# A hybrid mLSTM and Hyena block: MLP operand places opened from the start, the first mLSTM head begun beside the last value projections, and a new order from the mLSTM to the output projection

## The chip, the cores and the metric

The kernel runs on one core of a Trainium2 chip. A time is the device time of one execution in microseconds (us). The unchanged kernel took 2704.43 us, the median of three runs between 2702.84 and 2706.27.

## What is computed

One layer of an encoder on a sequence of 2048 rows and width 1024, in float32:

```python
hn = rms_norm(x, norm_mix_pre)
proj = hn @ w_in
cv = short_conv3(proj[..., :N_CONV], conv_w, conv_b)        # 2560 columns
q, k = heads(silu(cv[..., :512])), heads(silu(cv[..., 512:1024])) * 128 ** -0.5
v, o_gate = heads(proj[..., 2560:3072]), sigmoid(proj[..., 3072:3584])
gates = proj[..., 3584:3600] + b_gates                      # log i, log f, two directions, 4 heads
h_fwd = mlstm_chunkwise(q, k, v, gates[:, 0], log_sigmoid(gates[:, 1]))
h_bwd = flip(mlstm_chunkwise(flip(q), flip(k), flip(v), flip(gates[:, 2]), log_sigmoid(flip(gates[:, 3]))))
y_m = group_rms((h_fwd + h_bwd) * o_gate, 4, mlstm_norm_w)  # 512 columns
z = cv[..., 1024:1536]
for o in (0, 1):                                            # Hyena, FFT over twice the length
    z = cv[..., 1536 + 512 * o:2048 + 512 * o] * two_sided_fft_conv(z, filt[:, 0, o], filt[:, 1, o], fb[o])
y_h = group_rms(z, 8, hyena_norm_w)                         # 512 columns
x = x + rms_norm(concatenate([y_m, y_h]) @ w_out, norm_mix_post)
ff = square(relu(rms_norm(x, norm_mlp_pre) @ w_mlp_in)) @ w_mlp_out
x = x + rms_norm(ff, norm_mlp_post)
```

The mLSTM has 4 heads of 128 columns. It works in chunks of 128 rows, 16 to a head. Per chunk it needs a 128x128 score (q times k), weighted by an exponential of gate sums and masked to one side per direction; the product of these weights with v; and the product of q with a state that is carried from chunk to chunk, forwards and backwards.

## The kernel before

Every dense product in float32 is made of three matmuls on rounded parts (`mm3`, lines 159 to 161): an operand is split into a high and a low part (`split`, lines 166 on ScalarE and 169 on VectorE or GpSimd). The mLSTM's and the transposes' matmuls take plain float32, and the trace shows them as two matmuls each.

The stages in order of time: the normalised input is transposed and split into `hn` (16 tiles of rows, in four blocks of four); the convolved projections; the filters' spectra; then two things at once, the values' projection (four groups of 260 columns, 16 row tiles each, `values_project`) and the Hyena convolution (`hyena`). `drive(work, leads)` interleaves these two by costs: each step of the lead yields a number, and the values advance until their own yields have reached it. When the Hyena steps are done, `long_conv` closes its pools, opens the pools of the mLSTM (`mearly`, `mps0`), loads k, v and q of head 0, yields 14, waits until the gates are computed and turns the four groups of k (`turned`, line 945: four transposes; lines 950 and 952: weighted by the gates on ScalarE and VectorE into `kw`). All this stands in a manual schedule: the engines run in the written order.

Then comes `mlstm`, whose order a scheduler sets from the written one, by its own costs. After 15 `state_step`s of head 0 (line 966: two matmuls into `pv`; line 971: the state `st`, decayed, plus `pv`), 64 chunks run, head by head. `scores` makes `pS` (line 990) and two exponentials on ScalarE (line 993) of a tile `mb`, which is a broadcast row from memory, masked on GpSimd (lines 980 and 981). After every fourth chunk line 996 forms the weights `pm` of four chunks on VectorE. Five chunks later (LAG) `values` makes `ps` (q times state, line 1008) and `pa` (weights times v, line 1010). ScalarE scales `ps` into `nm` (1015), VectorE adds `pa` (1018), and after four chunks VectorE forms a quotient (1024 to 1026), GpSimd multiplies and adds the directions (1028 and 1030), and a DMA issued by ScalarE stores `ht` to `ym`. Such later pieces are put on a list and issued by `issue` in later chunks. In chunks 6 to 9 of a head the next head's k is turned, in chunks 8 to 15 its states are stepped, two a chunk.

From chunk 50 on, `loads_ahead` loads what the output projection needs first: rows of Hyena's output for row tile 0 and later 1, and the rows k = 4..7 of `w_out` into four buffers `wf4`..`wf7`, then k = 0..3. `first_gate` gates, norms and turns row tile 0 near the end.

`out_proj` is a generator over 16 row tiles. Before its loop it turns `w_out` into operands (`weight(k)`: line 1342 on ScalarE, 1343 on VectorE, with the norm's weights). A row tile needs `po`, two banks and 48 matmuls in all: 24 of the k = 4..7 half with Hyena's row (`gate`: line 1290 `py`, lines 1291 to 1300; turned by line 1306 into `yz`) and 24 of the k = 0..3 half with the mLSTM's row (`mixed`: load `ymt`, product with the output gate at line 1371, norm; turned into `ym`). `mixed(0)` must wait for the store of the mLSTM's last chunk. The MLP follows; of its operand places (tags `hm10` to `hm71`, 8 KB per partition each) those from `hm30` on lie in a pool that opens after the mLSTM.

The queue of DMAs issued by SyncE (SP) holds the loads in written order (`load`, line 231); ScalarE issues the stores (line 234), and waits there itself until the data are ready.

## Time and profile before

| | |
|---|---|
| median of three runs | 2704.43 us |
| the profiled execution | 2700.58 us |
| its span | 2698.5 us |
| PE, PEld, DVE, ACT, POOL busy | 96%, 78%, 57%, 46%, 45% |
| last value matmul begins | 1023.39 |
| first mLSTM output matmul (`ps`) | 1043.93 |
| last mLSTM output matmuls (`pa`) begin | 1166.82 |
| first turn of an mLSTM row (`ptp`) | 1193.72 |

PE is TensorE's matmuls, PEld its weight loads, DVE VectorE, ACT ScalarE, POOL GpSimd, SP SyncE; ACTq and SPq are their DMA queues. The last four rows are positions in the profiled execution, in us from the start of its span. A row of the timeline gives start, duration, engine, line, operation, and in brackets how long the engine had been idle and what it waited for. The duration of a matmul's record is longer than the distance of starts, since matmuls overlap in a pipeline; prices come from starts.

### The profile page before, as it was taken

The numbers are of one execution on the slowest core, as the hardware profiler recorded it, in microseconds if no ns is written. First come the engines' busy times: TensorE is split into PE (matmuls) and PEld (weight loads), VectorE is DVE, ScalarE is ACT, GpSimd is POOL, SyncE is SP. The second block draws the span as 40 slices with busy tenths as digits, with TensorE's granted clock in tenths as the row PEclk, the third lists the DMA queues.
The fourth block names the chain that finished last, engine by engine and source line by source line (L and its number), as shares of the span: only waits on it lengthen the run. The fifth ranks groups of instructions, "written<-read, shape, count | busy, mean of one in ns | idle before, by whom it ended". The sixth has DMA issues, their size and how long they took to land.

```text
span 2698.5 us, 35390 instructions
## 1 busy us (share of the span) xinstructions
PE 2598.6 (96%) x12237; PEld 2109.2 (78%) x12237; DVE 1541.0 (57%) x2454; ACT 1230.1 (46%) x2292; POOL 1206.1 (45%) x964
## 2 busy tenths in 40 slices
PE   6999999999999998879997999999999999999998
PEld 4778888777798888757774788868888888888876
DVE  5676653777556666656556444474444433543477
ACT  6355544555544446643334444454544333232344
POOL 1211114555225543456667877687772340301232
PEclk9999999999999999899999999999999999999999
DMA  6233336666676658546755444555447453445555
GB/s 173 56 93 110 113 117 216 187 196 187 198 237 180 197 167 272 183 152 213 245 186 210 156 141 163 185 190 172 144 156 282 146 181 98 129 144 160 183 168 214
DMA packets 288354, 465.74 MB, mean 173 GB/s; under 512 B 37542, under 2 KB 149414, under 8 KB 287152
## 3 DMA queue, kind: packets, MB, share of 16 engines
q1 hardware_dynamic: 227600, 324.85, 39.0%
q10 hardware_dynamic: 53264, 117.53, 11.4%
q0 software_dynamic: 7312, 21.11, 3.1%
q8 instruction: 97, 1.59, 0.2%
q14 instruction: 81, 0.66, 0.1%
HBM read 289.27 MB, written 174.13 MB: 172 GB/s over the span
## 4 chain that ended last, share of the span: by engine, by line
PE 39%; DVE 4%; POOL 4%; issue 3%; DMA 2%; ACT 2%; ACTq 0%; DVEq 0%; SPq 0%; POOLq 0%
PE pm L159 13%; PE pm L160 13%; PE pm L161 13%; DMA m<-in_w_mlp_out_dram 1%; POOL xt L1255 1%; DVE cb L169 1%; POOL cb L169 1%; ACT xo L1395 1%; DVE hm L1892 0%; DVE hm L169 0%; DVE xo L1398 0%; DMA hm<-ht 0%; DVE gss L1297 0%; POOL ht L1430 0%; DVE hm L1822 0%
## 5 line engine op out<-in xcount | busy, mean ns | idle before, releaser
L166 ACT CAST cb<-m 128x1024 fp32r<-128x1024 f32 (+1 forms) x342 | 277.4, 846 | 441.3 <-PE pm L159 386.2
L169 DVE TENSOR_TENSOR cb<-m,cb 128x1024 fp32r<-128x1024 f32 (+1 forms) x222 | 237.3, 1106 | 303.1 <-ACT cb L166 302.6
L160 PE MATMUL pm<-cb 128*128 128x512 f32 x880 | 343.4, 390 | 7.8 <-DVE cb L169 7.8
L159 PE MATMUL pm<-cb 128*128 128x512 f32 x880 | 342.3, 389 | 1.3 <-DVE cb L169 1.0
L159 PE MATMUL pm<-hm,cb 128*128 128x512 f32 x840 | 331.4, 394 | 12.3 <-DVE m L1703 6.4
L161 PE MATMUL pm<-cb 128*128 128x512 f32 x880 | 342.5, 389 | 0.0
L160 PE MATMUL pm<-hm,cb 128*128 128x512 f32 x840 | 330.2, 393 | 2.5 <-POOL hm L169 2.5
L161 PE MATMUL pm<-hm,cb 128*128 128x512 f32 x840 | 329.7, 393 | 0.0
L169 POOL TENSOR_TENSOR cb<-m,cb 128x1024 fp32r<-128x1024 f32 x120 | 266.1, 2230 | 57.5 <-ACT cb L166 57.5
L1703 DVE TENSOR_TENSOR m<-pm,m 128x512 f32<-128x512 f32 x224 | 153.9, 690 | 229.4 <-PE pm L161 220.5
L159 PE MATMUL pt<-hn,w 128*128 128x512 f32 x640 | 269.5, 421 | 1.0 <-ACT hn L486 0.9
L160 PE MATMUL pt<-hn,w 128*128 128x512 f32 x640 | 253.9, 397 | 0.7 <-DVE hn L487 0.7
L161 PE MATMUL pt<-hn,w 128*128 128x512 f32 x640 | 253.0, 395 | 0.0
L169 POOL TENSOR_TENSOR raw<-raw,hi 128x512 fp32r<-128x512 f32 x160 | 206.1, 1301 | 99.7 <-ACT hi L166 74.8
L160 PEld LDWEIGHTS pm<-cb 128*128 128x128 f32 x880 | 165.2, 188 | 45.7 <-DVE cb L169 11.7
L159 PEld LDWEIGHTS pm<-hm,cb 128*128 128x128 f32 x840 | 159.2, 189 | 49.0 <-POOL cb L169 7.6
L159 PEld LDWEIGHTS pm<-cb 128*128 128x128 f32 x880 | 165.1, 188 | 36.5 <-ACT junk L1877 1.4
L161 PEld LDWEIGHTS pm<-cb 128*128 128x128 f32 x880 | 165.2, 188 | 33.9
L160 PEld LDWEIGHTS pm<-hm,cb 128*128 128x128 f32 x840 | 159.4, 190 | 37.4 <-POOL hm L169 2.9
L161 PEld LDWEIGHTS pm<-hm,cb 128*128 128x128 f32 x840 | 159.2, 190 | 34.2
L1707 ACT ACTIVATE m<-m 128x512 f32<-128x512 f32 x128 | 80.7, 630 | 229.1 <-DVE m L1703 221.7
L635 POOL DMA_DIRECT2D vp<-vst x96 | 61.2, 642 | 231.7 <-ACT vst L631 230.6
(320 smaller groups left out, 5725.6 us busy)
## 6 DMA issues: line engine op xcount, KB each, us to landing
ga<-m ACTq DMA_DIRECT2D x96, 512.0 KB, 3.6
m<-ga SPq DMA_DIRECT2D x96, 512.0 KB, 3.8
d<-st ACTq DMA_DIRECT2D x64, 512.0 KB, 3.2
m<-in_w_mlp_in_dram SPq DMA_DIRECT2D x64, 512.0 KB, 5.7
m<-in_w_mlp_out_dram SPq DMA_DIRECT2D x114, 256.0 KB, 4.0
raw<-d SPq DMA_DIRECT2D x96, 256.0 KB, 2.9
xt<-in_x_dram SPq DMA_DIRECT2D x32, 512.0 KB, 3.9
dk<-kst SPq DMA_DIRECT2D x32, 512.0 KB, 4.0
```

What stands on the lines that cost most here:

```text
L159: pe.matmul(ps, w[1], x[0], start=first, stop=False)
L160: pe.matmul(ps, w[0], x[1], start=False, stop=False)
L161: pe.matmul(ps, w[0], x[0], start=False, stop=last)
L166: self.act.copy(hi, src)
L169: (eng_lo or self.dve).tensor_tensor(lo, src, hi.bitcast(F32), ALU.subtract)
L635: pool.dma_start(dst[:, 8 * b + e:8 * b + 8:2, cc:cc + 128], st[64 * e:64 * e + 64])
L1255: eng.tensor_tensor(res[:, cs], tmp[e], res[:, cs], ALU.add)
L1395: act.activation(x1, xt, AF.Square, accum_out=ss1[:, h:h + 1])
L1703: dve.tensor_tensor(dst, a, b, ALU.add)
L1707: act.activation(g, g, AF.Relu)
```

## The change

The pool `hq` of the MLP's places with tags 40 to 71 (eight of the fourteen; `hm30` and `hm31` go to a pool that opens later) is opened at the beginning. The first two blocks of `hn` live in those places, as halves of [128, 4, 512], so that `hn_tile`, `block` and `transpose_split` index halves. When these blocks have been read for the last time, during the last group of values, the places take head 0's and head 1's k, v, q and part of the `mb` tiles. Small constant tiles share one tile `cw` (`decay` among them).

During the last values group, steps t = 4 to 15 issue these loads and the masks of the first two `mb`. After Hyena (whose yields go from 1.3 to 1.2), `long_conv` yields 1.4 after each of: four turns, 15 state steps and four scores of head 0. The value matmuls between two of these number twelve.

`mlstm` runs under a manual schedule, begins at chunk 4, and gets written tables for its loads, turns, gates, and weights. The product `pm` is issued one chunk later than its last exponential, `scaled` at once. The four operands of `w_out` k = 4..7 are made inside head 3, from one buffer `wf` in place of four. Row tiles 0 and 1 are both gated there.

The border's order is written too: operands k = 0..3 alternate with the po of row tiles 0 and 1 (k = 4..7), then the po of row tile 2, then the first mLSTM row is turned.

VectorE from the values to the mLSTM (z is Hyena's; kw, st, pm belong to head 0, or to head 1 where kw follows pm), before:

```order
L1155 TENSOR_TENSOR z<-z,pu 128x512
L952 TENSOR_TENSOR kw_10341<-ptk,qt 128x512
L952 TENSOR_TENSOR kw_10353<-ptk,qt 128x512
L971 SCALAR_TENSOR_TENSOR st<-st,decay,pv 128x129 x3
L952 TENSOR_TENSOR kw_10365<-ptk,qt 128x512
L971 SCALAR_TENSOR_TENSOR st<-st,decay,pv 128x129 x5
L952 TENSOR_TENSOR kw_10377<-ptk,qt 128x512
L971 SCALAR_TENSOR_TENSOR st<-st,decay,pv 128x129 x22
L996 SCALAR_TENSOR_TENSOR pm<-pS,mb 128x1024
```

The same place, after:

```order
L1196 TENSOR_TENSOR z<-z,pu 128x512
L976 TENSOR_TENSOR kw_10134<-ptk,qt 128x512
L976 TENSOR_TENSOR kw_10160<-ptk,qt 128x512
L976 TENSOR_TENSOR kw_10185<-ptk,qt 128x512
L976 TENSOR_TENSOR kw_10212<-ptk,qt 128x512
L995 SCALAR_TENSOR_TENSOR st<-st,cw,pv 128x129 x30
L1030 SCALAR_TENSOR_TENSOR pm<-pS,hm_10084 128x1024
```

All four groups of kw now precede the first state.

ScalarE where the operands of w_out are made (wo and hm are the operands, ht the mLSTM's output), before:

```order
L1015 ACTIVATE nm<-ps,qt 128x129 x6
L234 DMA ym<-ht 128x4x128
L1015 ACTIVATE nm<-ps,qt 128x129 x2
L1342 ACTIVATE wo_11960<-wf_10390,yw 128x1024
L166 CAST y_10396<-pty 128x512
L1342 ACTIVATE wo_11960<-wf_10391,yw 128x1024
L1295 ACTIVATE rda<-yz 128x512
L234 DMA ym<-ht 128x4x128
L1342 ACTIVATE wo_11962<-wf_10392,yw 128x1024
L1342 ACTIVATE wo_11962<-wf_10393,yw 128x1024
```

The same operands, after:

```order
L1336 ACTIVATE hm_11366<-wf,yw 128x1024
L1027 ACTIVATE mb<-mb,qt 128x128 x2
L1055 ACTIVATE nm<-ps,qt 128x129 x2
L1027 ACTIVATE mb<-mb,qt 128x128 x2
L1055 ACTIVATE nm<-ps,qt 128x129 x2
L1336 ACTIVATE hm_11366<-wf,yw 128x1024
L234 DMA ym<-ht 128x4x128
L1027 ACTIVATE mb<-mb,qt 128x128 x2
L1055 ACTIVATE nm<-ps,qt 128x129 x2
L1027 ACTIVATE mb<-mb,qt 128x128 x2
L1055 ACTIVATE nm<-ps,qt 128x129 x2
L1336 ACTIVATE hm_11368<-wf,yw 128x1024
```

They stood behind the last scaling of the mLSTM and now stand between the exponentials and scalings of its last head.

SP's queue of loads in head 3, before (rd, xg, rda: Hyena's rows; mb: rows of the weights; wf, wfa: rows of w_out):

```order
L231 DMA rd_10394<-d_3601 128x2x512
L231 DMA xg_10395<-vp_76 128x1x512
L231 DMA wf_10390<-in_w_out_dram 128x1024
L231 DMA mb<-mrow 128x2x512
L231 DMA wf_10391<-in_w_out_dram 128x1024
L231 DMA mb<-mrow 128x2x512
L231 DMA wf_10392<-in_w_out_dram 128x1024
L231 DMA wf_10393<-in_w_out_dram 128x1024
```

After:

```order
L231 DMA rd_10524<-d_3610 128x2x512
L231 DMA xg_10525<-vp_75 128x1x512
L231 DMA mb<-mrow 128x2x512
L231 DMA hm_10399<-mrow 128x2x512
L231 DMA wf<-in_w_out_dram 128x1024
L231 DMA hm_10399<-mrow 128x2x512
L231 DMA wf<-in_w_out_dram 128x1024 x3
L231 DMA rda<-d_3610 128x2x512
L231 DMA wfa<-in_w_out_dram 128x1024 x4
```

Every load of wf has the same buffer for its target; behind the last of them stand the loads for row tile 1 and the other half of w_out.

The core of the diff:

```diff
@@ build: pools
+            self.hq = c.enter_context(tc.tile_pool(name="hq", bufs=1, reuse_waits="tile"))
-            self.hn = [[hp.tile([128, 8, 512], F32R, name=f"hn{b}{e}") for e in range(2)] for b in range(4)]
+            self.hn = [[[self.place(t) for t in tags[2 * e:2 * e + 2]] for e in range(2)]
+                       for tags in (("60", "61", "50", "51"), ("70", "71", "40", "41"))]
...
-            self.ahead = {k: op.tile([128, D], F32, name=f"wf{k}") for k in range(4, 8)}
...
-            self.mlstm()
+            with tc.manual_schedule():
+                self.mlstm()
...
-            for _ in range(6):
-                next(out)
+            next(out)
@@ long_conv
-        self.head_loads(0, "kvq")
-        yield 14.0
-        while not self.gates_done:
-            yield 1.0
-        for g in (0, 3, 1, 2):
-            self.turned(0, g)
-            yield 2.5
+        yield 1.4
+        for i, g in enumerate((0, 3, 1, 2)):
+            self.turned(0, g, ("kt", "s")[i % 2])
+            yield 1.4
+        for step in range(15):
+            self.state_step(0, step, self.mps0, ("s", "kt")[step % 2])
+            yield 1.4
+        for n in range(4):
+            self.scores(0, n)
+            yield 1.4
@@ values_project
+        first = {4: (self.head_loads, 0, "k"), 5: (self.head_loads, 0, "v"), 6: (self.weights_load, 0), 7: (self.head_loads, 0, "q"),
+                 8: (self.weights_load, 1), 9: (self.head_loads, 1, "k"), 10: (self.masked, 0), 11: (self.head_loads, 1, "v"),
+                 12: (self.masked, 1), 13: (self.weights_load, 2), 14: (self.weights_load, 3), 15: (self.head_loads, 1, "q")}
@@ mlstm
-        LAG, AHEAD = 5, 10
-        LOADS = {1: "v1", 5: "q1", 9: "k2", 14: "v2", 19: "q2", 32: "k3", 32 + LAG: "v3", 40: "q3"}
+        LAG = 5
+        LOADS = {4: (2, "k"), 8: (2, "v"), 12: (2, "q"), 28: (3, "v"), 32: (3, "k"), 37: (3, "q")}
+        WEIGHTS, AHEAD = (49, 51, 53, 56), (38, 46, 49, 51, 53, 55, 57, 58, 59, 60)
+        TURNS = ((5, 6, 7, 8), (3, 5, 6, 7), (5, 6, 7, 8))
+        GATES = {58: (0, 0), 59: (1, 0), 60: (0, 1), 61: (1, 1), 64: (0, 2), 66: (0, 3), 67: (1, 3)}
...
-        for n in range(64 + LAG):
+        for n in range(4, 64 + LAG):
...
+            self.issue(n)
...
+            if n % 4 == 3 and n // 4 + 1 < 16:
+                self.masked(n // 4 + 1)
+            if n in WEIGHTS:
+                self.weight(4 + WEIGHTS.index(n))
+            if n in AHEAD:
+                self.loads_ahead(AHEAD.index(n))
...
-            self.issue(n)
@@ scores
+        if i == 3:
+            if h + ch == 3:
+                weighted()
+            else:
+                self.later.append((self.now + 1, weighted))
@@ values
-        work = [scaled, sums] + ([last, None, stored] if i == 3 else [])
+        scaled()
+        work = [None, sums] + ([last, None, stored] if i == 3 else [])
@@ hyena, three places
-                    yield 1.3
+                    yield 1.2
@@ loads_ahead
         elif i < 5:
-            self.load(ahead[3 + i], self.io["w_out"][128 * (3 + i):128 * (4 + i), :])
+            ahead[3 + i] = self.mwk.tile([128, D], F32, tag="wf", name="wf", bufs=1)
+            self.load(ahead[3 + i], w[128 * (3 + i):128 * (4 + i), :])
@@ new
+    def weight(self, k):
+
+        hi, lo = (e[:, k % 2, :] for e in self.wos[k // 2])
+        wf = self.ahead.pop(k)
+        self.act.activation(hi, wf, AF.Copy, scale=self.yw[:, k:k + 1])
+        self.dve.scalar_tensor_tensor(lo, wf, self.yw[:, k:k + 1], hi.bitcast(F32), ALU.mult, ALU.subtract)
@@ out_proj
-        for k in (4, 5, 6, 7):
-            weight(k)
-            if k == 5:
-                zs[1] = gate(1)
-            yield
...
+        with tc.manual_schedule(engines={mybir.EngineType.PE,mybir.EngineType.DVE,mybir.EngineType.Activation}):
+            opened[2] = opening(2)
+            tiles = mixed_loads(0)
+            pos[0], pos[1] = banks(0), banks(1)
+            for k in (4, 5, 6, 7):
+                weight(k - 4)
+                for i in range(2):
+                    for e in range(2):
+                        part(pos[i], e, yz[i], 4, (k - 4,))
+                if k == 5:
+                    zs[2] = gate(2)
+
+            yz[2] = yz[0]
+            self.turn_split(ps.tile([128, 512], F32, tag="tp", name="ptp", bufs=3), zs.pop(2), yz[2])
+            pos[2] = [self.h1p.tile([128, 512], F32, tag="h1", name="po1"), ps.tile([128, 512], F32, tag="tp", name="po2", bufs=3)]
+            for e in range(2):
+                part(pos[2], e, yz[2], 4)
+            ym = {0: turned(mixed(0, tiles), 0, 1)}
```

213 lines of the change are left out of this document (110 added, 103 removed).

## The prediction

> **What bounds the kernel now.** I read the page first (PE busy 96% of the span, so only stretches where PE idles can give anything), then busy time in windows, then PE's own timeline at both ends of the mLSTM, then groups, waits and DMA there. In the windows the columns are the width, then busy PE, PEld, DVE, ACT, POOL, the granted clock, the DMA share and GB/s:
>
> ```profile
> 950.00:1000.00 50.00, 50.00 (x333) 44.07 (x333) 32.17 (x47) 25.79 (x58) 28.51 (x29) 1.00 0.58 186
> 1000.00:1050.00 50.00, 43.58 (x296) 39.07 (x295) 24.66 (x55) 23.73 (x73) 6.53 (x16) 0.93 0.68 225
> ...
> 1100.00:1150.00 50.00, 43.77 (x292) 39.21 (x290) 33.23 (x91) 31.41 (x110) 26.02 (x27) 0.93 0.42 124
> 1150.00:1200.00 50.00, 38.41 (x173) 29.20 (x174) 29.48 (x53) 24.66 (x53) 23.83 (x16) 0.90 0.47 143
> ```
>
> The values before 1000 keep PE full. From 1000 to 1050 and 1100 to 1200 it is busy 125.8 of 150, at a clock of 0.90 to 0.93: this is the stretch that the change rewrites. Its ends on PE:
>
> ```profile
> 1023.39 0.28 PE L161 MATMUL pt<-w,hn 128*128 128x260 f32 x1
> 1023.51 0.60 PE L945 MATMUL ptk<-eye,k 128*128 128x128 f32 x4
> 1026.85 0.97 PE L945 MATMUL ptk<-eye,k 128*128 128x128 f32 x4 [2.75 <-DVE kw L952]
> ...
> 1043.93 0.46 PE L1008 MATMUL ps<-st,q 128*128 128x258 f32 x1 [1.60 <-DVE st L971]
> ...
> 1166.82 0.61 PE L1010 MATMUL pa<-v,pm 128*128 128x129 f32 x4
> ...
> 1172.32 0.71 PE L159 MATMUL po<-wo,y 128*128 128x512 f32 x2 [3.03 <-DVE y L169]
> ...
> 1185.65 0.80 PE L159 MATMUL po<-wo,yt 128*128 128x512 f32 x1 [4.21 <-DVE yt L169]
> ...
> 1193.72 0.60 PE L1306 MATMUL ptp<-eye,ymt 128*128 128x128 f32 x4
> 1194.16 1.88 PE L1290 MATMUL py<-rd,s1i 128*128 128x512 f32 x4
> 1195.72 0.55 PE L159 MATMUL po<-wo,yt 128*128 128x512 f32 x1
> ```
>
> The last values matmul starts at 1023.4, the first mLSTM output (ps) at 1043.93, the last (pa) ends its issue at 1167.3, and the first turned mLSTM row (ptp from ymt) comes at 1193.72. So 170.2 us have three parts: **start-up** 20.4, **loop** 123.4, **border** 26.4. I price each part after the change, to the same amount of work.
>
> **Unit prices.** A plain chunk on PE, the step of a state (pv), and two output matmuls before and after the clock has come up, from starts:
>
> ```profile
> 1047.73 0.39 PE L966 MATMUL pv<-v,kw 128*128 128x129 f32 x2
> 1047.95 0.39 PE L990 MATMUL pS<-q,k 128*128 128x128 f32 x2
> ...
> 1151.08 0.71 PE L1010 MATMUL pa<-v,pm 128*128 128x129 f32 x4 [2.44 <-ACT nm L1015]
> 1151.63 0.39 PE L990 MATMUL pS<-q,k 128*128 128x128 f32 x2
> 1151.86 0.60 PE L1008 MATMUL ps<-st,q 128*128 128x258 f32 x2
> 1152.29 0.61 PE L1010 MATMUL pa<-v,pm 128*128 128x129 f32 x4
> 1152.74 0.39 PE L990 MATMUL pS<-q,k 128*128 128x128 f32 x2
> ...
> 1174.85 0.63 PE L161 MATMUL po<-wo,y 128*128 128x512 f32 x1
> 1175.28 0.63 PE L159 MATMUL po<-wo,y 128*128 128x512 f32 x1
> ...
> 1177.57 0.39 PE L159 MATMUL po<-wo,y 128*128 128x512 f32 x1
> 1177.80 0.39 PE L160 MATMUL po<-wo,y 128*128 128x512 f32 x1
> ```
>
> A chunk is 1.11 (1151.63 to 1152.74: pS 0.23, ps 0.43, pa 0.45); two records of pv are one float matmul and take 0.22, a state step of two directions 0.44; a transpose is 0.11 (four from 1193.72 to 1194.16); po is 0.23 warm and 0.43 cold; a row's py 1.6 (1194.16 to 1195.72). The other engines, by the groups of this stretch (busy, mean ns of one | idle before, releasers), then ACT's timeline in plain chunks and its longest wait:
>
> ```profile
> L971 DVE SCALAR_TENSOR_TENSOR st<-st,decay,pv 128x129 f32<-128x129 f32 x120 | 34.0, 344 | 12.5 <-PE pv L966 12.3
> L1028 POOL TENSOR_TENSOR nm<-nm,den 128x1024 f32<-128x1024 f32 x16 | 30.3, 1896 | 26.0 <-DVE den L1026 22.4 <-DMA mb<-mrow 2.3 <-PE ps L1008 1.3
> L996 DVE SCALAR_TENSOR_TENSOR pm<-pS,mb 128x1024 f32<-128x1024 f32 x16 | 19.5, 1217 | 2.6 <-PE pa L1010 2.6
> L950 ACT ACTIVATE kw<-ptk,qt 128x128 f32<-128x128 f32 x64 | 18.3, 376 | 9.8 <-PE ptk L945 9.7
> L1030 POOL TENSOR_TENSOR ht<-nm 128x512 f32<-128x512 f32 x15 | 16.3, 1092 | 0.7
> L993 ACT ACT_TABLE_LOAD x1 | 1.3, 1283 | 0.0
> ```
> ```profile
> 1144.64 0.69 ACT L993 ACTIVATE mb<-mb,qt 128x128 f32<-128x128 f32 x2 [1.25 <-POOL mb L980]
> ...
> 1145.74 0.69 ACT L993 ACTIVATE mb<-mb,qt 128x128 f32<-128x128 f32 x2
> ```
> ```profile
> ACT nm L1015 <- POOL ht L1030: 18.4, 8, 4.3
> ```
>
> ACT needs 1.10 for a plain chunk (1144.64 to 1145.74, two exps and two scalings, 0.28 each), as much as PE: nothing put on ACT inside the loop is free. The wait of 18.4 is ACT standing at the DMA ym<-ht, which it issues itself, until POOL's 1.90 and 1.09 are done; every exp and scaling queues behind it.
>
> **Start-up: 20.4 becomes 11.4.** Head 0's loads, 16 transposes and 12 of its 15 state steps move among the last value matmuls, 12 of these (0.12 each, 1023.39 to 1023.51, so 1.5 us) between two steps. They do not vanish: PE was full there, so it gets 16 x 0.11 + 24 x 0.22 = 7.0 longer. ACT and DVE are covered (25.8 and 32.2 of 50 before 1000); the order shows three extra table loads among the values, 3 x 1.28 of ACT's slack. What is left is bounded by ACT: a table load 1.28, eight exps of 0.28 (2.2), and 0.8 of a product of 1.22 that runs partly beside them: 4.3. If the step time of 1.5 does not cover the chain kw, pv, st (0.38 x 4 + 0.34 x 2 in DVE and ACT for the first, less for the next), it costs 3 more; if the eight exps are hidden, 2 less. Range 9 to 15.
>
> **Loop: 123.4 becomes 133.** The order of every engine is now as written, from chunk 4 on. 26 plain chunks at 1.15 (PE 1.11, ACT 1.10, almost no slack) are 29.9; 10 chunks that also turn a group at 2.2 (ACT 1.10 and four kw; four at 0.25 to 0.376 give 2.1 to 2.6, I take the low side since ACT issued exps every 0.28 above, though the records are longer) are 22; 2 that turn and step at 2.5, 5; 22 with two state steps at 2.28 (PE 1.11 + 0.88 = 1.99, plus a quarter of DVE's 1.22 product, which is now queued ahead of the sum that frees PE's banks), 50.2. That is 107; at PE's own time it would be 93; at 1.25, 2.6 and 2.6 (the engines delay one another by an eighth, kw at its mean, half the product uncovered) it is 121. The same prices put the old loop (34, 6, 6 and 18 of these, and a drain of 5 x 0.9) at 113, 10 below its 123.4, so about half of the 21.7 of ACT's waits for POOL (18.4 above, the rest at the exps) reached PE.
>
> Stores stay four chunks behind. Where chunks last 2.2, POOL's 3.0 fits; I leave 3.2 for heads 1 and 2, and 2 each for two stores in head 3, whose chunks are 1.15: 7.2 in all (0 to 16). New in head 3, priced by these rows (the tile wf in the old border, its loads from 1000 to 1200, and a row of that size from the page):
>
> ```profile
> L1342 ACT ACTIVATE wo<-wf,yw x4: 1136/1148/1164, 1169.8 to 1176.6; 128x1024 fp32r<-128x1024 f32 x4
> L1343 DVE SCALAR_TENSOR_TENSOR wo<-wf,yw,wo x4: 1233/1668/2110, 1172.1 to 1178.1; 128x1024 fp32r<-128x1024 f32 x4
> ```
> ```profile
> wf<-in_w_out_dram SPq DMA_DIRECT2D x4, 512.0 KB, 9.0
> ```
> ```profile
> xt<-in_x_dram SPq DMA_DIRECT2D x32, 512.0 KB, 3.9
> ```
>
> Four weights are turned into operands at chunks 49, 51, 53 and 56: 4 x 1.15 on ACT, 4.6. They share one buffer, so each load waits for the weight before it to have been read by ACT and then DVE: 1.15 + 1.5 + a landing. The trace has landings of 9.0 in a crowded stretch and 3.9 for such a load elsewhere; DMA is at 0.42 there and I take 3.9 plus 0.4 to issue, so a turn of the buffer lasts 6.9. Between the weights lie 3.4, 3.4 and 4.6 (two or three chunks and one weight): ACT waits 3.5 + 3.5 + 2.3, less 2.6 that PE's lag of five chunks and its banks absorb, 6.7. Behind ACT's weight stand the exps and scalings, behind these PE. On top: squares of two rows 1.1, one further weight 1.15, and a drain of 7 in which gates and py share the engines. 107 + 7.2 + 4.6 + 6.7 + 2.3 + 7 = 134.8, less 2 since the first chunk's pieces were counted at the start-up: 133.
>
> **Border: 26.4 becomes 13.8.** The old chain was store, load, product, norm:
>
> ```profile
> 1181.76 3.08 POOL L1371 TENSOR_TENSOR ymt<-ymt,ot 128x512 f32<-128x512 f32 x2 [1.55 <-DMA ymt<-ym]
> ...
> 1186.95 1.99 POOL L1300 TENSOR_TENSOR ymt<-ymt,gr_r 128x512 f32<-128x512 f32 x1 [2.11 <-DVE gr_r L241]
> ```
>
> From the last pa to ymt the chain is 1167.3 to 1188.9, 21.6; nothing in it is removed. But row 1 and four weights are ready now, so PE has 72 po (16.8), a py (1.6) and four transposes (0.44) ahead of the first ymt, 18.9 that start at once. POOL carries one gate less, so I put the chain at 19.5, plus 2 for a cold clock. Of what PE did there 24 po (5.6), py and a turn, 7.7, is work that before came after 1193.72: 19.5 + 2 - 7.7 = 13.8. With the chain at its old 21.6 it is 15.9.
>
> **Sum.** 11.4 + 133 + 13.8 = 158.2 against 170.2: 12 less. The profiled execution took 2700.6 (span 2698.5 and 2.1 around it); 2688.6 there, and with the 3.9 by which the median of the runs lies above it, **2692**. The Hyena stage's shorter pace (1.2 for 1.3) and the halved operand tiles cost nothing as long as PE stays full as at 950 to 1000, where DVE has 18 of 50 free; PE's instructions are the same number.
>
> The clock: PE started again without loss after one idle stretch, and not after another. After 2.44 idle (1151.08) the four pa take 0.55 and pS its warm 0.23. After 2.75 the four transposes last 0.97 (1026.85) for 0.60 (1023.51), and after 3.03 (1172.32) po starts lie 0.43 apart; some twelve po at +0.2 make 2.4 us. The Trainium skill ("TensorE: Matmul & The Clock Gate", What's actually happening) puts the drop to half clock after an idle window of about 3.4 us that runs freely. By it no stall of mine of 1 to 3 us need cool the clock, and the sum would lose its 2: 2690; the rows cool at 2.75 already, so I keep the 2.
>
> **Rivals.** *One buffer rules (slower).* If landings of wf stay at 9.0, each of three turns is 5.1 longer, 15.3; PE then idles over 2.75 three times and cools, 3 x 2.4 = 7.2: 12 gained become 10.5 lost, 2715. It decides from a landing of 7.9 without cooling (12 over three turns), 5.5 with it. For it: 9.0 is the only row of this transfer. Against it: DMA at 0.42 there, and four wf no longer side by side. *Written order eats it (no change).* Chunks at 121 for 107, or the stores at 16 with a few us more in chunks: 2702, within 5. For it: ACT and PE are both full in plain chunks, and an engine that waits in a fixed order makes the others wait. *Order is better than priced.* Chunks near PE's time (97 for 107), stores and buffer hidden (7 less): 2675. For it: the old loop lost time mostly to one wait, which a good order avoids. Should the early head 0 not start early (its loads queue behind the values' stores on SP), 8 come back: 2700, part of the no-change case.
>
> **Chances.** My forecast, 2684 to 2698: 0.46. Better, around 2675: 0.16. No change, around 2702: 0.19. Slower, around 2714: 0.19. 0.2%, 5.4 us, is about what this kernel's runs can tell from nothing. Faster 0.46 + 0.16 = 0.62, same 0.19, slower 0.19. The range 2676 to 2712 cuts off half of each outer case, 0.17; the likeliest case's own is 2684 to 2698.
>
> **What would show it.** Right: ps within 12 of the last value matmul; in head 3 three ACT waits for a DMA of wf of 2 to 4 each; no PE idle above 2 between the last pa and ptp from ymt, with po in the gap. Wrong: PE idle inside the values at ptk or pv (start-up), landings of wf over 6 and a clock of 0.5 in head 3 (slower), chunks with states above 2.4, or PE again waiting 4 for yt.

## The result and the profile after

The changed kernel took 2727.36 us (median of 4 runs, 2724.88 to 2731.86) against 2705.22 for the kernel before beside it: a ratio of 1.0083, 95% interval 1.007 to 1.0097, so about 22 us slower. 2692 was forecast. The profiled execution took 2724.88 with a span of 2722.9, 24.4 above the span before.

The windows of the rewritten stretch, after (columns as in the prediction):

```profile
1000.00:1050.00 50.00, 45.91 (x375) 44.41 (x375) 20.02 (x53) 28.28 (x80) 4.44 (x12) 1.00 0.77 224
...
1100.00:1150.00 50.00, 39.28 (x255) 35.65 (x254) 31.62 (x80) 32.36 (x104) 22.43 (x24) 0.90 0.54 156
1150.00:1200.00 50.00, 35.24 (x151) 25.57 (x150) 22.44 (x43) 23.89 (x58) 20.63 (x18) 0.85 0.48 162
```

PE is busier in the first row (45.91 for 43.58) at a full clock: the start-up became shorter. In the rows from 1100 to 1200 it is busy 74.5 of 100, where it was 82.2, at a lower clock. PE's timeline at the same places as before:

```profile
1033.64 0.28 PE L161 MATMUL pt<-w,hn 128*128 128x260 f32 x1
...
1037.09 0.60 PE L1048 MATMUL ps<-st,hm 128*128 128x258 f32 x2
...
1142.45 1.23 PE L1050 MATMUL pa<-v,pm 128*128 128x129 f32 x4 [4.93 <-DVE pm L1030]
1143.47 0.64 PE L1024 MATMUL pS<-hm,hm 128*128 128x128 f32 x2
...
1145.62 0.63 PE L1024 MATMUL pS<-hm,hm 128*128 128x128 f32 x2
...
1147.73 0.39 PE L1024 MATMUL pS<-hm,hm 128*128 128x128 f32 x2
...
1152.94 0.71 PE L1050 MATMUL pa<-v,pm 128*128 128x129 f32 x4 [2.18 <-ACT nm L1055]
1155.07 2.93 PE L1342 MATMUL py<-rd,s1i 128*128 128x512 f32 x3 [1.42 <-ACT nm L1055]
...
1177.66 0.97 PE L1050 MATMUL pa<-v,pm 128*128 128x129 f32 x4
...
1195.64 1.12 PE L1358 MATMUL ptp<-eye,yz 128*128 128x128 f32 x4 [3.03 <-POOL yz L1352]
1200.19 0.80 PE L159 MATMUL po<-hm,y 128*128 128x512 f32 x1 [3.44 <-DVE y L169]
...
1208.37 0.60 PE L1358 MATMUL ptp<-eye,ymt 128*128 128x128 f32 x4
...
1233.31 1.11 PE L1358 MATMUL ptp<-eye,ymt 128*128 128x128 f32 x4 [3.90 <-POOL ymt L1352]
```

The first mLSTM output follows the last value matmul by 3.45 us, where it was 20.5. But in the last head PE stands still for 4.93, 2.18 and 1.42, and after the last `pa`, where po should have filled the gap, for 3.03 and 3.44. The chunk from 1143.47 to 1145.62 takes 2.15, at a clock that has cooled, for 1.11 when warm.

To compare whole executions I counted PE's matmuls, each at its distance of starts when warm, and noted when the same amount of work was reached. Minus is earlier than before. `masklate`, `auto` and `lateswap` are experiments told of below:

| reached before at | place | after | masklate | auto | lateswap |
|---|---|---|---|---|---|
| 849 | Hyena and values | +3.9 | +4.6 | +3.4 | +4.2 |
| 1019 | end of the values | +3.2 | +2.6 | +2.3 | +3.5 |
| 1036 | start-up over | -3.8 | -4.4 | -4.7 | -3.5 |
| 1141 | in the last head | -7.9 | -16.4 | -10.5 | -15.6 |
| 1167 | end of the mLSTM | +7.6 | -5.3 | -9.3 | -11.4 |
| 1224 | first rows turned | +13.7 | +0.8 | -2.8 | -10.7 |
| 1245 | first row finished | +14.0 | +0.8 | -2.9 | -10.8 |
| 1501 | MLP begun | +18.9 | +6.4 | +2.3 | -7.8 |
| 2216 | first part of the MLP | +25.8 | +13.8 | +10.1 | -6.5 |
| 2688 | end | +24.5 | +12.9 | +9.6 | -5.5 |

So 3 to 4 us were lost while the values ran, 7 gained at the start-up and 4 in the next three heads; 15.5 were lost in the last head, 6 at the border, 5 up to the MLP and 7 in it. Each column is one profiled execution, and a figure beside one of PE's stalls can be off by 1. The forecast had named the loss in the last head as possible and sized it too small, had the border with the wrong sign, and did not have the MLP's at all.

### The profile page after: what moved, and what is told of

Same layout as the page of the kernel before. It is cut to its first block, busy times and chain, and to the rows that moved or that the text cites. A ratio compares the mean times of both kernels' runs of the same rounds, so it can differ in the third digit from the quotient of the medians.

```text
span 2722.9 us, 35360 instructions
## 1 busy us (share of the span) xinstructions
PE 2608.1 (96%) x12237; PEld 2110.3 (78%) x12237; DVE 1550.9 (57%) x2453; ACT 1235.2 (45%) x2295; POOL 1208.1 (44%) x964
## 4 chain that ended last, share of the span: by engine, by line
PE 53%; DVE 5%; POOL 5%; DMA 3%; ACT 3%; issue 3%; ACTq 0%; SPq 0%; DVEq 0%; POOLq 0%
PE pm L159 13%; PE pm L161 13%; PE pm L160 13%; PE pt L159 2%; PE pt L160 2%; PE pt L161 2%; PE pi L1218 1%; PE pm L157 1%; DVE cb L169 1%; POOL xt L1296 1%; PE pv L990 1%; ACT xo L1456 1%; DVE hm L1954 1%; POOL nm L1068 0%; DMA wf<-in_w_out_dram 0%
## 5 line engine op out<-in xcount | busy, mean ns | idle before, releaser
L159 PE MATMUL pm<-hm,cb 128*128 128x512 f32 x840 | 334.4, 398 | 13.8 <-POOL cb L169 7.4
L160 PEld LDWEIGHTS pm<-cb 128*128 128x128 f32 x880 | 165.2, 188 | 44.9 <-DVE cb L169 10.8
L613 DVE SCALAR_TENSOR_TENSOR yc<-pt,cw,yc 128x511 f32<-128x511 f32 (+1 forms) x280 | 135.1, 516 | 45.4 <-ACT yc L607 43.3
L1869 POOL TENSOR_TENSOR m<-m,hm 128x512 f32<-128x512 f32 x32 | 52.9, 1654 | 238.3 <-DMA m<-in_w_mlp_out_dram 232.6
L159 PE MATMUL pt<-hm,w 128*128 128x512 f32 x320 | 133.2, 416 | 1.1 <-ACT hm L495 1.1
```

The costliest lines, as they stand in the source:

```text
L159: pe.matmul(ps, w[1], x[0], start=first, stop=False)
L160: pe.matmul(ps, w[0], x[1], start=False, stop=False)
L613: dve.scalar_tensor_tensor(y[:, at], p[:, src], cw[:, ct, w:w + 1], y[:, at], ALU.mult, ALU.add)
L1869: pool.tensor_tensor(b[:, 0], b[:, 0], t2[s], ALU.subtract)
```

## The experiments

**One cause at a time.** Four kernels, each made for one suspect.

*align*: the operand places at other addresses. The change moved them: the eight places that it opens at the beginning lie at 32, 96 and 160 modulo 512 bytes within a partition, and at 416 before (from the allocation of the built programs; the traces hold no addresses). The MLP's other operand `cb` lies at 416. Here small constants are packed and two places allocated last, so that seven of the eight are at 416 again:

```diff
-            self.eps = cp.tile([128, 1], F32, name="eps")
+            sm = cp.tile([128, 16], F32, name="sm")
+            self.eps = sm[:, 14:15]
...
+            self.small = [sm[:, 8:10], sm[:, 10:12], cp.tile([8, 16, 2], F32, name="sr"), cp.tile([8, 17], F32, name="mr"),
+                          sm[:, 12:13], sm[:, 13:14]]
...
+            self.nw = sm[:, 0:8]
...
+            made = {t: self.place(t) for t in ("60", "61", "51", "70", "71", "41", "50", "40")}
+            self.hn = [[[made[t] for t in tags[2 * e:2 * e + 2]] for e in range(2)]
```

> The changed kernel with 128 bytes per partition taken out of the constants (small tiles packed into one) and the places 50 and 40 allocated last, so that seven of the eight MLP places that moved lie at 416 modulo 512 again, as the stationary tiles cb do; nothing else. Theory A, that the 11 us lost in the MLP come from where these places lie (1788 of the MLP's matmuls with a moving operand from a place start every 0.232 in the changed kernel, 0.227 in the one before): about 1560 matmuls x 0.0055 = 8.6 us less, 2719, and the spacing 0.227 again for places 41 to 71. Rival: the MLP is slower since its DMAs and weights come in another phase after a later start: spacing and time stay, 2727 within 3.

*beforepack*: the same packing in the kernel before, which moves its places off 416 (to 288).

> The kernel before with the same 128 bytes taken out of its constants, so that places 40 to 71 move from 416 to 288 modulo 512 and places 30 and 31 from 32 to 416; nothing else. Theory A: 1391 matmuls slow down by 0.0055 (7.6 us) and 336 become faster by the same (1.8): 5.8 us slower than the kernel before, 2711, all of it in the MLP. Rival (the addresses do nothing): 2705 within 2.

Align took 2723.88 (1.0069, 1.0054 to 1.0084); beforepack 2710.34 against 2705.51 (1.0016, 1.0007 to 1.0026): the old kernel becomes slower. The groups of an MLP window of 200 us in which PE never waits (PE's products of `hm` and `cb`; x is their number, then busy time, mean ns of one | idle before), before:

```profile
L160 PE MATMUL pm<-hm,cb 128*128 128x512 f32 x294 | 114.6, 390 | 0.0
L161 PE MATMUL pm<-hm,cb 128*128 128x512 f32 x293 | 114.3, 390 | 0.0
L159 PE MATMUL pm<-hm,cb 128*128 128x512 f32 x293 | 114.2, 390 | 0.0
```

After:

```profile
L161 PE MATMUL pm<-hm,cb 128*128 128x512 f32 x289 | 113.6, 393 | 0.0
L159 PE MATMUL pm<-hm,cb 128*128 128x512 f32 x288 | 113.6, 394 | 0.0
L160 PE MATMUL pm<-hm,cb 128*128 128x512 f32 x289 | 113.5, 393 | 0.0
```

Align:

```profile
L160 PE MATMUL pm<-hm,cb 128*128 128x512 f32 x293 | 114.3, 390 | 0.0
L161 PE MATMUL pm<-hm,cb 128*128 128x512 f32 x293 | 114.3, 390 | 0.0
L159 PE MATMUL pm<-hm,cb 128*128 128x512 f32 x292 | 114.1, 391 | 0.0
```

880 matmuls in 200 us before, 866 after, 878 in align: a matmul starts every 0.2273 us, 0.2309, 0.2278. In beforepack it is 869. PE never waits in any of the four and the granted clock is 1.00, so this is the matmul's own pace. From 1501 to 2216 of the table, after loses 7.0, align 0.8, beforepack 5.0. Addresses alone cost 5 to 7 us here. Align keeps only part of it in its time, because its lateness at the place 849 is 7.4 for after's 3.9. I put that down to the first constants sharing one tile; later kernels pack others.

*wf2*: two of the four weights of w_out get a buffer of their own.

```diff
-            ahead[3 + i] = self.mwk.tile([128, D], F32, tag="wf", name="wf", bufs=1)
+            if i == 2:
+                self.w40 = self.place("40", [128, 2, D], F32)
+            ahead[3 + i] = self.w40[:, i - 2] if i in (2, 3) else self.mwk.tile([128, D], F32, tag="wf", name="wf", bufs=1)
```

> The changed kernel with the loads of w_out rows k = 5 and 6 going to the two halves of place 40, which is free in head 3, so that none of the four loads waits for a weight to be made; k = 4 and 7 share the one buffer as before. Theory B, that the one buffer holds up head 3 (waits of 2.3 and 2.3 on ACT, 4.9 on PE behind them, a clock below 1): 8 to 12 us less, 2717, and no ACT wait for a DMA of wf. Rival: head 3 is held by POOL (masks of mb behind the quotients, 12.4 of ACT's waits): 3 us less at most, the waits for POOL growing by what the buffer's shrink.

2725.12 (1.0073, 1.0058 to 1.0088), 2 us less than after, which the intervals don't tell from nothing. In after, ScalarE's two waits are seen in its timeline, and so is a third of another kind:

```profile
1138.47 1.15 ACT L1336 ACTIVATE hm<-wf,yw 128x1024 fp32r<-128x1024 f32 x1 [2.32 <-DMA wf<-in_w_out_dram]
...
1144.57 1.15 ACT L1336 ACTIVATE hm<-wf,yw 128x1024 fp32r<-128x1024 f32 x1 [2.34 <-DMA wf<-in_w_out_dram]
...
1150.80 0.37 ACTq L234 DMA_DIRECT2D ym<-ht  x1
1151.38 0.40 ACT L1027 ACTIVATE hm<-hm,qt 128x128 f32<-128x128 f32 x1 [3.48 <-POOL hm L1014]
```

In wf2 the later of the two waits for `w_out` is gone, but the first is there still, at the same place. Its load has a place of its own and went out earlier, at 1131.72, but did not land earlier:

```profile
1139.61 1.15 ACT L1338 ACTIVATE hm<-hm,yw 128x1024 fp32r<-128x1024 f32 x1 [2.32 <-DMA hm<-in_w_out_dram]
```

So wf2 did not take away what it was made to take away, and PE's wait at the `pa` behind it is 4.94 as before. How that wait hangs on the load is seen on VectorE in after:

```profile
1139.66 1.60 DVE L1337 SCALAR_TENSOR_TENSOR hm<-wf,yw,hm 128x1024 fp32r<-128x1024 f32 x1 [3.24 <-ACT hm L1336]
1141.18 1.21 DVE L1030 SCALAR_TENSOR_TENSOR pm<-pS,mb 128x1024 f32<-128x1024 f32 x1
```

The product `pm` that PE's 4.93 waits for had its last exponential at 1135.6. It stood behind the low half of a weight, which waits for ScalarE's high half, and that for the load.

*bpool*: GpSimd joins the border's written order.

```diff
-        with tc.manual_schedule(engines={mybir.EngineType.PE,mybir.EngineType.DVE,mybir.EngineType.Activation}):
+        with tc.manual_schedule(engines={mybir.EngineType.PE,mybir.EngineType.DVE,mybir.EngineType.Activation,mybir.EngineType.Pool}):
```

> The changed kernel with GpSimd in the border's written order too, so that the norm of row tile 2's yz stands ahead of the product of ymt, which waits for a load. Theory C, that row 2's turn was late (PE idle 3.0 and 3.4 and cold) only because its norm stood behind that product on GpSimd: yz is turned some 5 us earlier, its 24 po fill the time to the first ymt, 7 us less, 2720. Rival: the chain store, load, product, norm of ymt sets the end of the border in any case: PE idles in one piece in front of the turn of ymt, 2 us less or nothing.

2727.47 (1.0083, 1.0068 to 1.0098), no gain. GpSimd's gate of row tile 2 now comes early and PE turns it at 1192.34 without idling; but PE then waits longer for the next thing:

```profile
1192.34 0.60 PE L1358 MATMUL ptp<-eye,yz 128*128 128x128 f32 x4
1199.74 0.80 PE L159 MATMUL po<-hm,y 128*128 128x512 f32 x1 [6.81 <-DVE y L169]
```

ScalarE in the same kernel shows why:

```profile
1197.86 0.63 ACT L1347 ACTIVATE ot<-ymt 128x512 f32<-128x512 f32 x1 [6.38 <-POOL ymt L1432]
1198.40 0.57 ACT L166 CAST y<-ptp 128x512 fp32r<-128x512 f32 x1
```

The square of the mLSTM's row, which waits for a store, a load and a product, stands ahead of the cast that PE needs, though the border's code has the cast first. The turn belongs to one written block and the square to the next, and the two blocks were mixed.

**The last head and the border's order.** *h3* issues the masks two chunks earlier and loads three of the four weights before their chunks; *mask1* has the masks alone; *oneblock* puts the mLSTM, the border and the first row tile into one written order.

```diff
-        WEIGHTS, AHEAD = (49, 51, 53, 56), (38, 46, 49, 51, 53, 55, 57, 58, 59, 60)
+        WEIGHTS, AHEAD = (49, 51, 53, 56), (38, 39, 40, 41, 52, 55, 57, 58, 59, 60)
...
-            if n % 4 == 3 and n // 4 + 1 < 16:
+            if n % 4 == 1 and n // 4 + 1 < 16:
                 self.masked(n // 4 + 1)
```

(h3 has this and wf2's edit; mask1 the last line alone.)

> The changed kernel with two things moved in the mLSTM: the masks of a group of mb issued two chunks earlier (ahead of the quotients of the group before on GpSimd), and the loads of w_out k = 4 to 6 issued at chunks 39 to 41 (two of them into place 40, which is free then), k = 7 at 52. Theory B2, that head 3 is held by both the buffer and the masks that wait behind the quotients (taking the buffer away alone left the masks): ACT's waits for masks and for w_out all but vanish and 7 us or more of head 3's 15 come back, 2720. Rival: the product of four chunks stands only one chunk ahead of its first use, so that any wait of ACT, that for the stores too, still stops PE: 3 us or less, 2724.

> The changed kernel with the masks of a group of mb issued two chunks earlier, and nothing else. The run h3, which had the earlier loads of w_out too, gained 7.9 us, the buffer's run 2.2. If masks and loads each hold head 3 by themselves, the masks alone give 2 to 4 us and ACT then waits for w_out instead; if the masks are the whole of it, they give 6 to 8.

h3 took 2719.48 (1.006, 1.0044 to 1.0077), mask1 2723.58 in a single execution: 8 and 4 less than after. The 4 is uncertain, since that one execution lies 1.3 under the fastest of after's four. The waits of ScalarE for GpSimd in the mLSTM (total, times, longest), after:

```profile
ACT hm L1027 <- POOL hm L1014: 7.1, 5, 3.5
ACT mb L1027 <- POOL mb L1014: 5.3, 5, 1.7
```

The same view of mask1:

```profile
ACT hm L1027 <- POOL ht L1070: 5.0, 3, 3.3
ACT mb L1027 <- POOL ht L1070: 4.4, 5, 1.5
```

The wait did not go. Its releaser changed from the mask (L1014) to `ht` (L1070), for which the store waits that stands ahead of the exponentials in ScalarE's queue.

```diff
-            with tc.manual_schedule():
-                self.mlstm()
+            self.border = ExitStack()
+            self.border.enter_context(tc.manual_schedule())
+            self.mlstm()
...
-        with tc.manual_schedule(engines={mybir.EngineType.PE,mybir.EngineType.DVE,mybir.EngineType.Activation}):
+        with ExitStack():
...
+            with self.border if i == 0 else tc.manual_schedule(engines={mybir.EngineType.PE,mybir.EngineType.DVE,mybir.EngineType.Activation}):
```

> The changed kernel with one written order from the mLSTM to the end of the first row of the output projection, for every engine, in place of three written blocks that the scheduler may shift against one another. Theory C2, that the border is late since pieces of a later block stand ahead of an earlier one's (the square of row 1's ymt ahead of the split of row 2's yz on ScalarE, two operands of w_out ahead of the last quotient on VectorE): the split of yz follows its turn at once, PE's idle 6.8 in front of row 2's po shrinks below 2, the first turn of ymt comes 7 us earlier, 2720. Rival: with four weights now behind the last quotient, PE waits for them and for the chain of ymt instead: 2 us or less.

2725.84 (1.008, 1.0065 to 1.0095). The stretch from the last `pa` to the first turned row fell from 29.9 to 23.7, so the mixing of blocks cost 6. But of the 4.8 us that this row then came earlier than in after (1203.53 for 1208.37) nothing was left at the place 1245 (+14.5, for +14.0): the time went again at a later row.

*pace13* gives Hyena its old pace:

```diff
-                    yield 1.2
+                    yield 1.3
```

> The changed kernel with Hyena's three yields at 1.3 as before the change. Theory D, that the shorter pace puts Hyena's splits ahead of the scaling of the values' weights on GpSimd and so costs the 4 us lost between 795 and 820: they come back, but Hyena ends some 10 us later (of 18 won) and head 0's steps no longer all fit beside the values: start-up 3 to 6 us longer, in sum 2727 within 3. Rival: the loss there has another cause and stays, and the start-up gets longer: 2731.

2729.76 (1.0093, 1.0078 to 1.0109), not better than after. The loss at the place 849 falls from 3.9 to 0.7, but the start-up is 0.0 instead of -3.8: Hyena ends 20 us later (last inverse transform at 1018.76 for 998.80), and head 0 has no value matmuls left to lie among. The loss among the values is real, and was paid back.

*combo* joins h3, oneblock and another packing that keeps the first constants in their own tiles:

```diff
-            self.small = [cp.tile(shape, F32, name=name) for name, shape in (
-                ("st", [128, 2]), ("ms", [128, 2]), ("sr", [8, 16, 2]), ("mr", [8, 17]), ("gm", [128, 1]), ("dc", [128, 1]))]
+            sm = cp.tile([128, 23], F32, name="sm")
+            self.small = [sm[:, 17:19], sm[:, 19:21], cp.tile([8, 16, 2], F32, name="sr"), sm[0:8, 0:17], sm[:, 21:22], sm[:, 22:23]]
```

> The changed kernel with the changes of the runs h3 and oneblock together, and seven of the eight moved places at 416 modulo 512 again, this time by packing only the gates' small tiles (the packing with the norm's weights cost 3 us at the start). If the three causes add up: 6 for the places, 7 for head 3, 7 for the border, 2707, no slower than the kernel before. Rival: what one frees another wait takes, 2715.

2713.18 (1.0032, 1.0019 to 1.0044). From the place 1501 to 2216 it loses 1.1, where after lost 7.0, so this packing holds. Still slower than before.

**Is the written order the cause?** *auto* leaves the mLSTM to the scheduler, all else as changed.

```diff
-            with tc.manual_schedule():
-                self.mlstm()
+            self.mlstm()
```

> The changed kernel with the mLSTM left to the scheduler again, with all the rest as changed (loads, turns, gates, weights in head 3, first head begun in the values). Theory E, that the written order as such is no loss (heads 0 to 2 are 4 us better than before) and head 3 loses by what was put there: 2727 within 4. Rival, that the fixed order makes the engines wait for one another: 8 us less or more, 2719, and most of it in head 3.

2710.05 (1.0023, 1.0014 to 1.0033): 17 us of the loss gone by this one edit. The last `pa` begins at 1159.81 instead of 1178.31, with the one buffer for w_out still there. So the loss in the last head is the written order's. Which part of it, the next runs tell.

*late* is combo with the store of the mLSTM's output one chunk later; *lateonly* is the changed kernel with that alone; *masklate* the changed kernel with that and mask1's line.

```diff
-        work = [None, sums] + ([last, None, stored] if i == 3 else [])
+        work = [None, sums] + ([last, None, None, stored] if i == 3 else [])
```

> The kernel combo with the store of every mLSTM group issued one chunk later. In combo ACT still waits 21.6 us between 1030 and 1182 at the stores for GpSimd, with exponentials and scalings behind. Theory F: these waits vanish and PE's waits for pm, nm and kw (17 us) shrink by half: 6 us less than combo, 2707. Rival: the waits are slack, since PE waits for VectorE's products and turns (kw): 2 us or less.

> The changed kernel with the store of every mLSTM group issued one chunk later, and nothing else. Theory H: store and masks are two places at which ScalarE stands for the same GpSimd work (the masks stand behind the products on GpSimd, the exponentials behind the store on ScalarE); the masks moved alone gave 4 and left the store, so the store moved alone leaves the masks: 4 us less at most, 2724, though the two together gave more than their sum (combo to late 15). Rival: the store alone was the cause, and moving it gives 10 or more, 2717.

> The changed kernel with the masks two chunks earlier and the stores one chunk later, and nothing else (loads of w_out, border and places as changed). Theory H: the two together free ScalarE, where alone the masks gave 4 and the stores 1; with the one buffer of w_out still in place, 10 to 14 us less, 2715. Rival: they add up to 5 as alone, and what late gained over combo needed the buffer or the border too: 2722.

late took 2698.19 (0.9971, 0.9961 to 0.9981), 15 less than combo. lateonly took 2726.49 (1.0075, 1.0056 to 1.0094), nothing, and masklate 2712.29 (1.0027, 1.0018 to 1.0036), 15 less than after. Alone the two edits are worth 4 (of one execution) and 1, together 15. lateonly's waits show the mask again:

```profile
ACT hm L1027 <- POOL hm L1014: 6.8, 4, 3.5
```

and in masklate neither remains:

```profile
ACT hm L1336 <- DMA wf<-in_w_out_dram: 6.9, 3, 3.0
...
ACT hm L1336 <- POOL ht L1070: 1.0, 1, 1.0
```

The waits for the mask and for the store lay side by side in one chain, and either alone held it. GpSimd's rows of after at that place:

```profile
1147.70 1.90 POOL L1068 TENSOR_TENSOR nm<-nm,den 128x1024 f32<-128x1024 f32 x1 [7.51 <-DVE den L1066]
1149.67 1.09 POOL L1070 TENSOR_TENSOR ht<-nm 128x512 f32<-128x512 f32 x1
1150.72 0.63 POOL L1014 TENSOR_SCALAR_AFFINE_SELECT hm<-hm 128x512 f32<-128x512 f32 x1
```

GpSimd had been idle for 7.51, not busy: the mask at 1150.72 stood behind a quotient whose sums were not there yet, and VectorE's part of that quotient stood behind the low half of the next weight (1145.75, idle 2.69 for ScalarE's high half). ScalarE's store went out at 1150.80, just after `ht` ended (1150.76), and its exponential at 1151.38, after the mask. Behind it stand the scalings, which PE's next `pa` needs. In masklate the waits for wf are longer (6.9) than in after, and it is still 15 faster; so those 15 did not need them to go.

They have a price of their own, though. By the table masklate has 8.5 of its gain before the last head (-16.4 for -7.9 at the place 1141) and still loses 11 in it, where after loses 15.5. PE's waits for `pm` from 1030 to 1182 in after, masklate and lateswap (a kernel told of below; it has masklate's two edits and h3's loads):

```profile
PE pa L1050 <- DVE pm L1030: 7.3, 4, 4.9
PE pa L1050 <- DVE pm L1030: 7.5, 3, 5.3
PE pa L1052 <- DVE pm L1032: 4.9, 4, 2.6
```

The loop, from the first `ps` to the end of the last `pa`, in one profiled execution of each:

| kernel | masks earlier | store later | loads of `w_out` ahead | loop, us |
|---|---|---|---|---|
| before | | | | 123.4 |
| after | no | no | no | 141.4 |
| lateonly | no | yes | no | 139.9 |
| mask1 | yes | no | no | 137.5 |
| h3 | yes | no | yes | 135.9 |
| masklate | yes | yes | no | 127.8 |
| late | yes | yes | yes | 120.8 |

With masks and store out of the way, the loads are worth 5 to 7 of the loop; while the store's wait is still there (mask1 to h3) they seem worth 1.6. ScalarE waits for no load of `w_out` in late. It has oneblock's order and combo's packing too; oneblock alone does not shorten the loop (142.1), but combo's is 2.1 under h3's, so up to 2 of the 7 may be theirs. So three waits lay side by side, not two, and the last head's loss is for a good part that of the loads.

**The border again.** In combo and late PE idles later, at the third turned row of the mLSTM. *lateswap* moves one line of late, *pmnow* also issues the product `pm` at once.

```diff
                     ym[1] = turned(ys.pop(1), 1, 1)
-                    zs[3] = gate(3)
                     ys[2] = mixed(2)
+                    zs[3] = gate(3)
```

> The kernel late with the mLSTM row 2 (product, norm) ahead of Hyena's row 3 in the written order of the first row of the output projection. Theory G, that the work done ahead at the border (24 po of row 2) only moves PE's wait to the turn of row 2's ymt (3.8 us and a cold clock in combo), which stands behind row 3's norm on GpSimd: 3 to 4 us less than late. Rival: row 3 is late then in its place: 1 us or less.

```diff
         if i == 3:
-            if h + ch == 3:
-                weighted()
-            else:
-                self.later.append((self.now + 1, weighted))
+            weighted()
```

> The kernel lateswap with the product pm issued at once after its last exponential, as before the change, and not one chunk later. PE waits 4.9 us in four places for that product in lateswap. If the lead of one chunk is too short, these waits shrink and 2 to 4 us are won, 2691; rival: VectorE then waits for the exponentials itself, the sums that free PE's banks come later behind it, and it loses 2 to 6, 2698.

PE's row and GpSimd's rows of combo:

```profile
1210.67 1.11 PE L1362 MATMUL ptp<-eye,ymt 128*128 128x128 f32 x4 [3.82 <-POOL ymt L1356]
```
```profile
1205.17 1.04 POOL L1356 TENSOR_TENSOR yz<-yz,gr_r 128x512 f32<-128x512 f32 x1 [5.82 <-DVE gr_r L241]
1206.17 1.27 POOL L1436 TENSOR_TENSOR ymt<-ymt,ot 128x512 f32<-128x512 f32 x1
```

GpSimd waits 5.82 for the norm of row 3's gate before it touches row 2's product, which PE needs first. With the two exchanged (lateswap):

```profile
1195.70 0.60 PE L1362 MATMUL ptp<-eye,ymt 128*128 128x128 f32 x4
...
1207.86 1.11 PE L1362 MATMUL ptp<-eye,ymt 128*128 128x128 f32 x4 [3.84 <-POOL ymt L1356]
```

The idle before the third turned row is gone; one of 3.84 stands at the fourth. lateswap took 2693.59 (0.9956, 0.9941 to 0.9972): about 11 us faster than the kernel before, and 34 faster than the change as made. pmnow took 2694.68 (0.9968, 0.9957 to 0.9979), the same as lateswap within the intervals; the delay of `pm` was worth nothing measurable.

## Why the prediction was wrong

In its own terms, from the starts quoted there and above (loop: ps to the end of the last `pa`'s issue, 1178.45, worked out like the 1167.3 of before; their last record starts at 1178.31; border: from there to the first turned mLSTM row; the next two rows go by the first output of the row loop, which comes 13.7 later than before, after a turned row 14.65 later, and by the spans):

| step | predicted | measured | off by |
|---|---|---|---|
| values before the start-up | 0 | +3.25 | +3.3 |
| start-up, 20.4 becomes | 11.4 | 10.45 | -1.0 |
| loop, 123.4 becomes | 133 | 141.4 | +8.4 |
| border to the first turned row, 26.4 becomes | 21.5 | 29.9 | +8.4 |
| work done ahead, given back | -7.7 | -0.9 | +6.8 |
| rest, up to the end | 0 | +10.7 | +10.7 |

The sum of the last column is 36.6; from -12 forecast to +24.4 in the spans it is 36.4.

**Start-up: right.** The last value matmul is 10.25 later, of which 7.0 was priced as the work put among the values; ps comes 13.7 after the old end of the values, 10.45 without their own lateness of 3.25. PE stood idle for kw twice among the values, 0.45 and 0.59 at a `pv`, the sign named for a wrong start-up, but too short to matter. The 1.79 that it waits for the first product comes just after ps and so falls into the loop here.

**Hyena's pace: wrong, small.** "Cost nothing as long as PE stays full" left out that GpSimd's splits for Hyena now come closer together and stand ahead of the scaling of the values' weights. ScalarE there in after:

```profile
812.02 0.62 ACT L166 CAST w<-wf 128x520 fp32r<-128x520 f32 x1 [4.93 <-POOL wf L552]
```

PE is busy 15.95 of the 20 us from 800. In pace13 the loss at this place is gone (0.7 for 3.9 at the place 849), and so is the start-up's gain.

**Loop: the term that failed is "Stores stay four chunks behind: 7.2 in all (0 to 16)".** It priced a store that waits for GpSimd's busy 3.0, and had no term for the masks, though the rows shown with it hold a wait of 1.25 for one (`mb L980`). In the written order a mask also stands behind the quotient, and the quotient waits for sums that ScalarE's own scalings feed, so ScalarE waited for itself by way of GpSimd. With masks earlier and the store later the loop is 127.8 (masklate: ps 1036.54, last `pa` 1164.19), so the two cost 13.6 together, where 7.2 stood for them.

The term for the single buffer of w_out, 6.7, was near in size: with the loads ahead as well the loop is 120.8 (late), 7.0 less, with the reserve made above. The division goes by this order of taking the waits away; in another order each looks small. The way from there to PE was wrong: the term went by ScalarE's exponentials and scalings, and the longest stall came by VectorE, where `pm` stands behind the weight's low half. So the near hit is partly luck. Its three waits were put at 3.5, 3.5 and 2.3; in after two came, of 2.32 and 2.34, in masklate three, of 6.9 together. Without both terms my sum is 119.1, 2 less than late's loop: chunks, states, weights and drain were right as a sum, and were not measured one by one. In after the second load took 3.2 from its issue to ScalarE's start, near the 3.9 taken:

```profile
1135.31 12.08 SPq L231 DMA_DIRECT2D wf<-in_w_out_dram  x3
```

(three loads from 1135.31 on; ScalarE starts on the first of them at 1138.47). The Trainium skill ("DMA: Bandwidth & Descriptors", Anatomy of one DMA), in a section on DMAs that GpSimd issues, says that any wait for a semaphore happens on the issuing sequencer, since DMA engines do not wait on semaphores. ScalarE's store is of another path, and agrees: at 1150.80, with everything behind it held until then.

**Border: "I put the chain at 19.5, plus 2" failed.** It took 29.9. bpool's rows and oneblock's 23.7 show the reason for 6 of the 8.4: the work that should fill the gap, row tile 2's turn and po, was itself queued behind the mLSTM row that it should cover, since separate written blocks were mixed. That the 24 po were written ahead of the turned row I had read from PE's order alone; ScalarE's and GpSimd's orders decided it. **"7.7 is work that before came after"** failed as well: work done ahead is kept only while something else is ready. The next rows' norms were not, so PE idled at them: 3.90 at 1233.31 in after, 3.82 in combo. lateswap removed one of these idles (5 us in the table from late's -6.2 to -10.8 at the place 1245), not the last one; the credit never came back in any run.

**The places: "the halved operand tiles cost nothing as long as PE stays full" failed** by the 7 us of the MLP: PE stays full there, and each matmul is 1.6% slower. The other 5 between the places 1245 and 1501 occur in every variant, beforepack among them (+4.2), and are not explained; some of it may be the one profiled execution of before, which lies 4 under its median.

**The rivals.** "Written order eats it" had the right mechanism, an engine that waits in a fixed order and makes the others wait, but stopped at 2702. auto, masklate and late confirm it at 15 to 17 us. "One buffer rules" had the right sign and came nearest in size (2715), by luck: it rests on landings of 9.0, which were 3.2 in after. The buffer does take part, but its waits as they were priced stood in the forecast already. Of what was to show the forecast right, one of three held in full (ps close behind the values), one in part (two waits for wf of 2 to 4, not three), and the third, no idle above 2 at the border, did not.

**The clock** was the small term "plus 2": it cooled in the last head too. In windows of 4 us, after (the number after the engines is the granted clock):

```profile
1144.00:1148.00 4.00, 4.00 (x18) 3.63 (x18) 2.18 (x6) 3.33 (x9) 0.30 (x1) 0.54 0.01 2
1148.00:1152.00 4.00, 2.76 (x20) 2.19 (x18) 1.64 (x3) 0.43 (x2) 3.86 (x4) 1.00 0.97 312
1152.00:1156.00 4.00, 1.64 (x5) 1.02 (x6) 1.96 (x4) 4.00 (x13) 0.00 (x0) 0.81 1.02 373
1156.00:1160.00 4.00, 4.00 (x14) 2.35 (x13) 1.52 (x4) 1.31 (x5) 3.56 (x4) 0.76 0.63 236
```

So the stall of 4.93 cost its own length and then half speed for about as long again: the two chunks from 1143.47 to 1147.73 took 4.26 for 2.22 when warm. The loop's price of each wait left that out.

## What to carry to other kernels

Where an order is written out, price it per engine queue: a short instruction that someone needs soon (a mask, a store's issue, a cast) must not stand behind a long one whose input comes late, and where several such waits lie side by side, each alone seems worth next to nothing until the others are gone; and see in the trace that an experiment took away the wait that it was made for. Work that fills a gap is worth what it says only if its own helpers on the other engines are ahead of what it covers, and if the thing after the gap is ready sooner too. Moving long-lived tiles moves their addresses: compare the distance of matmul starts before and after, even where the engine never waits.

## What the runs showed of the hardware

- The pace of a matmul of 512 columns depended on where its operands lie. With `hm` and `cb` both at 416 modulo 512 bytes 880 start in 200 us, with eight of the places at 32 to 160 866, with the places at 288 869 and with most back at 416 878, at full clock and with PE never waiting. That equality modulo 512 is the rule is the reading of these four layouts of one product, and isn't shown beyond them; why it is so stays open.
- The length of one idle stretch did not decide whether the clock cooled. In after, two of 2.18 and 1.42 that followed each other within 4 us cooled it (0.81 and 0.76 from 1152 to 1160). Before, one of 2.44 alone did not cool it and one of 2.75 did; in masklate one of 2.40 alone did (0.80 from 1144 to 1148). In all 17 traces the clock is at 1.0 or at 0.5, and each stretch of one clock lasts a whole number of times 3.41 us. I cut the traces into windows on that grid. A window at full clock in which PE was idle for more than 2.01 us in sum was never followed by another at full clock, and one with less than 1.35 idle always was; in between both occur. The 2.18 and 1.42 give 2.70 in one window (1151.09 to 1154.50), the 2.40 gives 2.13, and the 2.44 falls into two windows, with 1.30 and 1.14. The Trainium skill ("TensorE: Matmul & The Clock Gate", What's actually happening) asks for an idle window of about 3.4 us that runs freely. The grid agrees; but the windows with 2.70 and 2.13 were not idle as a whole, so here about 2 us of idle time in one was enough.
